# Block inverse of a chunked RWKV-7 scan: 128-row transposes and copies, and PSUM columns of its own for the third stage

## The chip, the cores and the metric

The kernel runs on one core of a Trainium2 chip. The metric is device time in microseconds for one execution. Every program is timed several times and the median counts. One further execution is recorded by the hardware profiler. It gives the trace from which all durations below are read.

## The reference, cut to what matters

One step of a two-layer trunk. Layer 0 is attention (differential heads and latent heads); layer 1 is a bidirectional RWKV-7 time mixing with 32 heads of width 64, over 512 latent tokens and 128 context tokens. The change touches layer 1 alone. Its recurrence, for each direction:

```python
def step(s, inp):
    r_t, w_t, k_t, v_t, kk_t, a_t = inp
    sa = jnp.einsum('bhij,bhj->bhi', s, -kk_t)
    s = s * w_t[:, :, None, :] + sa[..., None] * (kk_t * a_t)[:, :, None, :] + v_t[..., None] * k_t[:, :, None, :]
    return s, jnp.einsum('bhij,bhj->bhi', s, r_t)
...
s_fin, ys = lax.scan(step, s0, xs, reverse=reverse)
```

The kernel works on chunks of 64 tokens. Inside a chunk the `sa` terms of all tokens depend on each other through a strictly lower triangular 64x64 matrix, so each chunk and head needs the inverse of a unit lower triangular 64x64 matrix. That inverse is what the changed function computes.

## The kernel before, in words

Layer 1 runs over 16 pairs of heads and, for each, two passes u = 0 and 1: 32 **units**. A unit holds, in its 128 rows, both directions (64 rows each) for five chunks of two heads, so ten 64x64 inverses per direction.

For each unit the generator `unit` (L1488) writes out the work of three neighbouring units in one order. First comes the sequential scan of unit n (`stage_c`, L1299), then the list `P2` (L1482): the inverse of unit n+1 (`inv`), transposes of its keys (`bk`), its values (`pre`), a bonus term, and the Gram matrices of unit n+2 (`a2`, matmul L1125, evacuated by VectorE into GG at L1129). Between these steps `fill` lets the big projections (`project_steps`, matmul L126) advance by a few matmuls, as cover for the waits. The instruction order of TensorE is the order of this program text (`manual_schedule`, L1552); a scheduler orders VectorE, ScalarE and GpSimd by their priorities and its own estimate of time. Inverse steps are written with a raised priority (`urgent`, L1463).

The inverse (`stage_inv`, L1240) starts from 16x16 blocks already inverted on VectorE (tile DD) and has four steps, all of whose matmuls write into one PSUM tile, CC (128 rows x 2 banks x 512 columns):

- stage 1: 80 matmuls (L1260) into columns PB (416:496), then two VectorE operations (L1263) that make t16;
- stage 2: 80 matmuls (L1269) into columns PA (256:416), the inverses of the 32x32 diagonal blocks. Of each group of 64 rows the first 32 hold the upper block, the last 32 the lower. The upper ones are transposed by VectorE (L1274, two instructions of 32 rows, into DD), the lower ones copied by ScalarE into the result tile xd (L1276, two of 32 rows);
- stage 3: 40 matmuls (L1282) into the lower rows of the same columns PA. ScalarE then copies these (L1285, twice 32 rows) and the upper blocks (L1287, twice 32 rows);
- stage 4: 40 matmuls (L1291) into the upper rows of PA, then two ScalarE copies with scale -1 (L1294).

The scan of the next unit reads xd (matmul L1343).

CC is allocated at L848, right after layer 0's output projection and the modulation of layer 1's input. That modulation ends with VectorE operations at L818, which write h0lo, half of the input of every layer 1 projection. CC is first used as the accumulator of a projection: L911 sets up three projections lg[0], lg[1] (into tiles of the pool pj) and lg[2] (into CC), and L913 runs their weight chunks in turn, while VectorE is still writing the last parts of h0lo. A weight chunk is 12 pairs of matmuls of 320 columns. Each chunk of weights is split into two parts, whi by ScalarE (L100) and wlo by GpSimd (L101); wlo has two buffers.

Of the kernel before, what the change touches and what calls it, by code (L numbers as in the profile page):

```python
# [14 lines left out]
AF = mybir.ActivationFunctionType  # L15
# [38 lines left out]
def kernel(  # L54
# [5 lines left out]
    act, dve, pool, pe = nc.scalar, nc.vector, nc.gpsimd, nc.tensor  # L60
# [779 lines left out]
    with ExitStack() as l1:  # L840
# [5 lines left out]
        pc = tc.alloc_tile_pool(name="pc", bufs=1, space=PSUM)  # L846

        CC = pc.tile([128, 2, 512], F32, name="CC")  # L848

        def c3(t):  # L850
            return t.rearrange("p (c t) -> p c t", t=64)
# [7 lines left out]
        nlow = b1.tile([128, 1], F32, name="nlow")  # L859
        dve.tensor_reduce(out=nlow, in_=i32[:, 16:32], axis=AX.X, op=ALU.add, negate=True)  # L860
        i32b = i32.rearrange("p (o t) -> p o t", o=1).to_broadcast([128, 10, 32])
        t16 = b1.tile([128, 10, 32], F32, name="t16")
# [11 lines left out]
        for t in Xds:  # L874
            dma(out=t.rearrange("p c -> (p c)").rearrange("(p c) -> p c", p=128),
                in_=xds[0][:, 0:5, :].rearrange("p q t -> p (q t)"))
# [9 lines left out]
        def shifted(alloc, wd, n, ti, pt=None, lead=False):  # L886
            if pt is None:
                pt = pj.tile([128, 1024], F32, tag="pj", name="pj")
            yield from project_steps([pt[:, 512 - HT:512], pt[:, 512:512 + HT]], wd, KT, n, h1hi, h1lo, HALVES, 4, 0, lead)
            X = pt[:, 512 - HT:512 + HT]  # L890
            out = alloc()
            act.activation(out=out, in_=X[:n], func=AF.Copy, scale=c0[:n, ti:ti + 1])
            for a, b, _ in SEGS:
                dve.scalar_tensor_tensor(out=out[:, a + 1:b], in0=X[:n, a:b - 1], scalar=V("mu0", ti)[:n],
                                         in1=out[:, a + 1:b], op0=ALU.mult, op1=ALU.add)
                dve.scalar_tensor_tensor(out=out[:, a:b - 1], in0=X[:n, a + 1:b], scalar=V("mu1", ti)[:n],
                                         in1=out[:, a:b - 1], op0=ALU.mult, op1=ALU.add)

            return out
# [8 lines left out]
        def ring(pool_, tag, shape=(128, T), dt=F32, **kw):  # L908
            return lambda: pool_.tile(list(shape), dt, tag=tag, name=tag, **kw)

        lg = [shifted(ring(u1, tag), w_l1[64 + j], 128, 64 + j, pt, j < 2)  # L911
              for j, (tag, pt) in enumerate((("az", None), ("kk", None), ("kzs", CC.rearrange("p b c -> p (b c)"))))]
        for j in (0, 1, 0, 1, 2) + (0, 1, 2) * 3:  # L913
# [124 lines left out]
        def halves_of(u):  # L1038
            return [(hf ^ u, HT * hf, HT * hf + HT, 5 * hf, 5 * hf + 5) for hf in range(2)]
# [200 lines left out]
        def stage_inv(i, u):  # L1240
            un = units[(i, u)]
            zh = halves_of(u)
            G = un.GAq
            xd = un.xd = xds[u]
            Dn, D = un.DD[:, 0], un.DD[:, 1]
            grp = [(64 * z + 32 * m, 32 * m, 2 * ca) for z, _, _, ca, _ in zh for m in range(2)]
            PA, PB = CC[:, :, 256:416], CC[:, :, 416:496]

            def blk(o, q):
                return PA[o:o + 32, q // 5, 32 * (q % 5):32 * (q % 5) + 32]  # L1250

            def pa(o):
                return PA[o:o + 32].rearrange("p b (q t) -> p b q t", t=32)

            def b2(t):
                return t.rearrange("p (b q) t -> p b q t", b=2)

            for q in range(10):
                for o, col, q0 in grp:
                    pe.matmul(PB[o:o + 32, q // 5, 16 * (q % 5):16 * (q % 5) + 16], G[o:o + 32, q0 + q, col:col + 32],  # L1260
                              Dn[o:o + 32, q, 0:16], start=True, stop=True, tile_position=(o, o))
            for k in range(2):
                dve.scalar_tensor_tensor(out=t16[:, 5 * k:5 * k + 5, 0:16],  # L1263
                                         in0=PB[:, k].rearrange("p (q t) -> p q t", t=16), scalar=nlow,
                                         in1=i32b[:, 0:5, 0:16], op0=ALU.mult, op1=ALU.add)
            yield
            for q in range(10):
                for o, col, q0 in grp:
                    pe.matmul(blk(o, q), t16[o:o + 32, q, :], D[o:o + 32, q, :],  # L1269
                              start=True, stop=True, tile_position=(o, o))  # L1270
            xn = un.DD[:, 0]
            for o, col, q0 in grp:
                if col == 0:
                    dve.transpose(out=b2(xn[o:o + 32]), in_=pa(o))  # L1274
                else:
                    act.activation(out=b2(xd[o:o + 32, :, col:col + 32]), in_=pa(o), func=AF.Copy)  # L1276
            yield
            t32 = xn
            for q in range(10):
                for z, a, b, ca, cb in zh:  # L1280
                    o = 64 * z
                    pe.matmul(blk(o + 32, q), G[o:o + 32, 2 * ca + q, 32:64], xn[o:o + 32, q, :],  # L1282
                              start=True, stop=True, tile_position=(o, o + 32))
            for o in (0, 64):
                act.activation(out=b2(t32[o + 32:o + 64]), in_=pa(o + 32), func=AF.Copy)  # L1285
            for o in (0, 64):
                act.activation(out=b2(xd[o:o + 32, :, 0:32]), in_=pa(o), func=AF.Copy)  # L1287
            yield
            for q in range(10):
                for o in (0, 64):  # L1290
                    pe.matmul(blk(o, q), t32[o + 32:o + 64, q, :], xd[o + 32:o + 64, q, 32:64],  # L1291
                              start=True, stop=True, tile_position=(o + 32, o))
            for o in (0, 64):
                act.activation(out=b2(xd[o:o + 32, :, 32:64]), in_=pa(o), func=AF.Copy, scale=-1.0)  # L1294
            yield

        carry = {}
# [1 line left out]
        def stage_c(i, u):  # L1299
# [3 lines left out]
            Yn = un.Yn = u1.tile([128, 5, 2, 64], F32, tag="yz", name="Yn")  # L1303
            Ys = CC[:, :, 192:512].rearrange("p h (s d) -> p s h d", d=64)

# [13 lines left out]
            for s in range(5):  # L1319
                loc = (s, 4 - s)  # L1320
                cgs = (un.ca[0] + loc[0], un.ca[1] + loc[1])
                if u == 0 and s == 0:
                    dma(out=ZS[:, 0, :], in_=state[0, i])
                    dma(out=ZS[:, 3, :], in_=state[1, i])
                    S = ZS[:, 0:2, :]
                C = CC[:, :, 0:64]
                pu, pn = (CC[:, 1, 64:192], CC[:, 0, 64:192]), CC[:, 0, 64:192]
                if s:
# [159 lines left out]
        def unit(n):  # L1488
# [5 lines left out]
            sub, a1, kk = of(stage_a3, n + 1), of(stage_a1, n + 2), kk_of(n + 2)  # L1494
            gn = stage_gn(*seq[n - 1]) if n else iter(())
            bonus, inv = of(stage_bonus, n), urgent(of(stage_inv, n + 1))
            P1 = {-1: [kk], 2: [gn, sub, kk], 4: [a1], 5: [kk, sub], 7: [a1], 8: [gn], 10: [a1], 11: [gn], 13: [a1], 15: [bonus]}
            w1 = 0
# [27 lines left out]
        def prologue():  # L1526
            quota[1] = 1.0
            need(proj_k, 0)
            script(dict(kk=kk_of(0), a1=of(stage_a1, 0)),
                   (("a1", 9), ("a1", 9), ("kk", 9), ("kk", 7), ("a1", 7), ("kk", 5), ("a1", 0)))  # L1530
            need(proj_r, 0)
            all_(of(stage_e, 0))
            fill(36)
            a1, bk = of(stage_a1, 1), of(stage_bk, 0)
            a2 = of(stage_a2, 0)
            for g, w in ((a2, 4), (a1, 6), (a2, 4), (a1, 6), (a2, 4)):
                step(g)
                fill(w)
            all_(a2, of(stage_a3, 0))
            for g, w in ((bk, 6), (bk, 6), (a1, 8), (bk, 6)):  # L1540
                step(g)
                fill(w)
            all_(a1, bk)
            need(proj_v, 0)
            all_(of(stage_e, 1))
            of(stage_v, 0)
            script(dict(pre=of(stage_pre, 0), inv=urgent(of(stage_inv, 0)), a2=of(stage_a2, 1)),
                   (("pre", 6), ("pre", 32), ("inv", 3), ("a2", 6), ("inv", 3), ("inv", 3),
                    ("a2", 6), ("pre", 3), ("inv", 3), ("pre", 3), ("a2", 6)))
            need(proj_r, 1)  # L1550
# [139 lines left out]
```

## Time and profile before

| | us |
|---|---|
| median of 3 runs | 3641.58 (3637.04 to 3645.55) |
| profiled execution, own time | 3634.34 |
| its span, first to last instruction | 3632.5 |
| TensorE busy | 3426.5 (94%) |
| VectorE busy | 2141.9 (59%) |
| ScalarE busy | 1632.0 (45%) |
| GpSimd busy | 1190.0 (33%) |
| mean granted TensorE clock | 0.988 of full speed |

PE is TensorE's matmul stream and PEld its weight loads, DVE is VectorE, ACT is ScalarE, POOL is GpSimd, SP issues DMAs. In a timeline row the columns are start, duration, engine, line, operation, output tile <- input tiles, shapes, count; a bracket at the end gives how long the engine had been idle before it and who ended that wait. Rows of neighbouring equal instructions are merged, so a duration there runs from the start of the first to the end of the last.

### The profile page before, as it was taken

The page shows a single profiled execution, that of the slowest core. Times are in us where ns is not written, and L with a number is a line of the kernel's source. Part 1 is how long each engine was busy: PE and PEld are TensorE (multiplying, and loading weights), DVE is VectorE, ACT ScalarE, POOL GpSimd, SP SyncE. Part 2 cuts the span into 40 slices and gives each one's busy share as a digit, 9 for nine tenths or more (in the row PEclk, how much of TensorE's full clock was granted, in tenths as well). Part 3 has the DMA queues.
Part 4 walks back from the last instruction along what each step waited for, and adds up shares of the span by engine and source line. Part 5 has one row for each costly group of instructions (what it writes and reads, how often), then busy time and mean ns, then how long its engine had stood idle before and what let it go on. Part 6 is the DMA issues. An engine that isn't in the chain of part 4 may idle for free. (4 is left out here: it accounts for less than half of the span.)

```text
span 3632.5 us, 84033 instructions
## 1 busy us (share of the span) xinstructions
PE 3426.5 (94%) x34432; PEld 2997.9 (83%) x34432; DVE 2141.9 (59%) x4249; ACT 1632.0 (45%) x3342; POOL 1190.0 (33%) x1094
## 2 busy tenths in 40 slices
PE   8999999999999989999999999999999999999998
PEld 4788889988888879898877778778777787888898
DVE  3356655666666584555666666666676666665402
ACT  3244443444444422444544545545545455555422
POOL 1222112222222344542333323333233333333444
PEclk9999999999999999999999999999999999999999
DMA  9623433333333364332222222222222322323534
GB/s 332 220 69 103 124 96 113 106 110 108 107 107 110 119 221 162 106 94 64 69 72 62 68 70 69 67 67 69 68 68 66 74 65 68 75 70 92 172 96 145
DMA packets 388610, 376.23 MB, mean 104 GB/s; under 512 B 200512, under 2 KB 242560, under 8 KB 388224
## 3 DMA queue, kind: packets, MB, share of 16 engines
q1 hardware_dynamic: 388224, 370.86, 34.7%
q8 instruction: 270, 4.42, 0.5%
q14 instruction: 116, 0.95, 0.1%
HBM read 328.51 MB, written 42.24 MB: 102 GB/s over the span
## 5 line engine op out<-in xcount | busy, mean ns | idle before, releaser
L101 POOL TENSOR_TENSOR wlo<-raw,whi 128x512 fp32r<-128x512 f32 (+1 forms) x628 | 861.2, 1372 | 1976.3 <-PE pj L126 1254.4
L126 PE MATMUL pj<-h0hi,wlo 128*128 128x320 f32 x4448 | 1085.2, 323 | 20.2 <-POOL wlo L101 20.2
L126 PE MATMUL pj<-h0hi,whi 128*128 128x320 f32 x4448 | 1081.0, 322 | 2.3 <-ACT whi L100 1.8
L126 PE MATMUL pj<-h0lo,whi 128*128 128x320 f32 x4448 | 1075.4, 321 | 2.3 <-DVE h0lo L101 1.6
L126 PEld LDWEIGHTS pj<-h0hi,wlo 128*128 128x128 f32 x4448 | 744.2, 190 | 56.4 <-POOL wlo L101 24.8
L126 PEld LDWEIGHTS pj<-h0hi,whi 128*128 128x128 f32 x4448 | 743.1, 190 | 36.0 <-issue 7.9
L126 PEld LDWEIGHTS pj<-h0lo,whi 128*128 128x128 f32 x4448 | 745.7, 190 | 30.6 <-issue 8.2
L100 ACT ACTIVATE whi<-raw 128x512 fp32r<-128x512 f32 (+1 forms) x628 | 390.7, 622 | 743.1 <-PE pj L126 402.3
L200 DVE SCALAR_TENSOR_TENSOR aacc<-araw,scs,aacc 128x512 f32<-128x512 f32 x480 | 409.5, 901 | 16.6 <-DMA araw<-in_dram 15.8
L364 DVE TENSOR_REDUCE nm<-S 128x1 f32<-128x768 f32 (+1 forms) x120 | 98.3, 819 | 255.2 <-PE S L376 255.1
L1345 ACT ACTIVATE UV<-CC 64x128 f32<-64x128 f32 x160 | 43.1, 269 | 335.6 <-PE CC L1343 306.8
L724 DVE SCALAR_TENSOR_TENSOR x<-pj,mod,xr 128x512 f32<-128x512 f32 (+2 forms) x68 | 33.2, 524 | 248.1 <-PE pj L126 242.6
L367 ACT ACTIVATE P<-S,nm 128x768 f32<-128x768 f32 (+1 forms) x120 | 95.1, 792 | 166.7 <-DVE nm L364 166.0
L1129 DVE TENSOR_TENSOR GG<-gram,con 128x512 f32<-128x512 f32 (+1 forms) x192 | 107.4, 595 | 73.6 <-PE gram L1125 73.2
L1125 PE MATMUL gram<-AR,BK 64*128 64x128 f32 x1280 | 114.0, 292 | 18.0 <-DVE GG L1129 13.2
L1125 PEld LDWEIGHTS gram<-AR,BK 64*128 64x128 f32 x1280 | 90.3, 189 | 42.7 <-DVE GG L1129 24.1
L1061 PE MATMUL plo<-lr,lw 96*128 96x320 f32 x256 | 103.7, 487 | 5.7 <-DMA lr<-lorad 4.7
L566 PE MATMUL po<-PT,vt 128*128 128x128 f32 x800 | 103.2, 276 | 0.1
L566 PEld LDWEIGHTS po<-PT,vt 128*128 128x128 f32 x800 | 98.0, 191 | 4.2 <-issue 2.5
L1359 DVE TENSOR_TENSOR S<-CC,S 128x128 f32<-128x128 f32 (+1 forms) x112 | 29.9, 267 | 118.8 <-PE CC L1310 78.6
L1335 DVE SCALAR_TENSOR_TENSOR rhs<-CC,MV 128x128 f32<-128x128 f32 x160 | 45.8, 286 | 69.9 <-PE CC L1333 69.6
L1343 PEld LDWEIGHTS CC<-rhs,xd 64*64 64x64 f32 x1280 | 49.8, 133 | 42.8 <-DVE rhs L1335 20.8
(338 smaller groups left out, 5209.1 us busy)
## 6 DMA issues: line engine op xcount, KB each, us to landing
raw<-in_dram SPq DMA_DIRECT2D x612, 256.0 KB
araw<-in_dram SPq DMA_DIRECT2D x384, 256.0 KB
lr<-lorad SPq DMA_DIRECT2D x128, 120.0 KB
Ld<-GG SPq DMA_DIRECT2D x64, 160.0 KB
lw<-in_dram SPq DMA_DIRECT2D x128, 48.0 KB
x<-in_dram SPq DMA_DIRECT2D x16, 320.0 KB
xr<-in_dram SPq DMA_DIRECT2D x16, 320.0 KB
DD<-Xd SPq DMA_DIRECT2D x32, 160.0 KB
```

What stands on the lines that cost most here:

```text
L100: act.activation(out=hi, in_=src, func=AF.Copy)
L101: (lo_eng or pool).tensor_tensor(out=lo, in0=src, in1=rf(hi), op=ALU.subtract)
L126: pe.matmul(p[:n, 0:b - a], w, x[:, kk ^ flip, a:b], start=(kk == order[0] and i == 0), stop=(kk == order[-1] + kc - 1 and i == 2))
L200: dve.scalar_tensor_tensor(out=acc[:, s], in0=raw, scalar=scs[:, k, s:s + 1], in1=acc[:, s], op0=ALU.mult, op1=ALU.add)
L364: dve.tensor_reduce(out=nm, in_=S[:, 0:nk], axis=AX.X, op=ALU.max, negate=True)
L367: act.activation(out=P[:, 0:nk], in_=S[:, 0:nk], func=AF.Exp, bias=nm, accum_out=l)
L566: pe.matmul(po[:, 0:128], H.vt[:, kt, :], PT[:, j, :], start=(j == 0), stop=(j == n - 1))
L1061: pe.matmul(ps[:, 0:HT], lw, lo, start=True, stop=True)
L1125: pe.matmul(ps[:, j * 128:(j + 1) * 128], BK[hs, c + j, :, :].rearrange("p a t -> p (a t)"), AR[hs, c + j, :, :].rearrange("p a t -> p (a ...
L1129: dve.tensor_tensor(out=GG[:, c:c + n, h, :], in0=ps[:, 0:n * 128].rearrange("p (j t) -> p j t", t=128), in1=maskg.rearrange("p (o t) -> p ...
L1335: dve.scalar_tensor_tensor(out=rhs.rearrange("p (h d) -> p h d", h=2), in0=C, scalar=-1.0, in1=un.MV[:, s, :].rearrange("p (h d) -> p h d" ...
L1343: pe.matmul(pu[z][o:o + 64, hs], xd[o:o + 64, 2 * loc[z] + h, :], rhs[o:o + 64, hs], start=True, stop=True)
```

## The change

Four things change. The second-stage transposes become one instruction over all 128 rows and the second-stage copies one, so rows that were not needed are processed too (the lower blocks are transposed into rows of DD that are overwritten later, the upper ones copied into a part of xd that is overwritten by stage 4). Stage 3 writes to columns PT (0:160) of CC instead of PA; its result and the upper blocks are copied by one 128-row instruction each, and the minus sign moves to the first of them. As the second copy now also writes 32 rows per direction of xd that must be zero, two GpSimd memsets of 32 rows set them back. Stage 4's result is copied by one 128-row instruction. Since rows of PT that no matmul has written are now read, the whole of CC is set to zero once, where it is allocated.

```diff
         CC = pc.tile([128, 2, 512], F32, name="CC")
+        dve.memset(CC, 0.0)
...
-            PA, PB = CC[:, :, 256:416], CC[:, :, 416:496]
+            PA, PB, PT = CC[:, :, 256:416], CC[:, :, 416:496], CC[:, :, 0:160]
...
-            xn = un.DD[:, 0]
-            for o, col, q0 in grp:
-                if col == 0:
-                    dve.transpose(out=b2(xn[o:o + 32]), in_=pa(o))
-                else:
-                    act.activation(out=b2(xd[o:o + 32, :, col:col + 32]), in_=pa(o), func=AF.Copy)
+            xn = t32 = un.DD[:, 0]
+            dve.transpose(out=b2(xn), in_=p4(PA))
+            act.activation(out=b2(xd[:, :, 32:64]), in_=p4(PA), func=AF.Copy)
             yield
-            t32 = xn
             for q in range(10):
                 for z, a, b, ca, cb in zh:
                     o = 64 * z
-                    pe.matmul(blk(o + 32, q), G[o:o + 32, 2 * ca + q, 32:64], xn[o:o + 32, q, :],
+                    pe.matmul(blk(PT, o + 32, q), G[o:o + 32, 2 * ca + q, 32:64], xn[o:o + 32, q, :],
                               start=True, stop=True, tile_position=(o, o + 32))
-            for o in (0, 64):
-                act.activation(out=b2(t32[o + 32:o + 64]), in_=pa(o + 32), func=AF.Copy)
-            for o in (0, 64):
-                act.activation(out=b2(xd[o:o + 32, :, 0:32]), in_=pa(o), func=AF.Copy)
+            act.activation(out=b2(t32), in_=p4(PT), func=AF.Copy, scale=-1.0)
+            act.activation(out=b2(xd[:, :, 0:32]), in_=p4(PA), func=AF.Copy)
+            for o in (32, 96):
+                pool.memset(xd[o:o + 32, :, 0:32], 0.0)
             yield
...
-            for o in (0, 64):
-                act.activation(out=b2(xd[o:o + 32, :, 32:64]), in_=pa(o), func=AF.Copy, scale=-1.0)
+            act.activation(out=b2(xd[:, :, 32:64]), in_=p4(PA), func=AF.Copy)
```

The remaining lines of the diff only rename: `blk` takes the columns as an argument, and `p4` replaces `pa`.

The instructions move at two places. The first is ScalarE's row around the inverse of one unit, where L1276, L1285, L1287 and L1294 of the kernel before are L1273, L1280, L1281 and L1289 of the changed one; the bracket names what an instruction waits for. Before:

```order
L1276 ACTIVATE xd_14636<-CC 32x10x32 [waits DVE_49]
L1200 ACTIVATE BKn<-pbk 128x512 [waits PE_49]
L1276 ACTIVATE xd_14636<-CC 32x10x32 [waits DVE_49]
L1222 ACTIVATE UV<-pvt 64x512 [waits PE_49]
L1222 ACTIVATE UV<-pvt 64x512
L100 ACTIVATE whi<-raw 128x512 [waits DMAHW4_49,PE_49,Pool_49]
L1285 ACTIVATE DD<-CC 32x320 [waits DMAHW5_49,PE_49]
L1285 ACTIVATE DD<-CC 32x320
L1287 ACTIVATE xd_14636<-CC 32x10x32 x2
```

And now:

```order
L1273 ACTIVATE xd_14637<-CC 128x10x32 [waits DVE_49]
L1201 ACTIVATE BKn<-pbk 128x512 [waits PE_49]
L1223 ACTIVATE UV<-pvt 64x512 [waits PE_49]
L1223 ACTIVATE UV<-pvt 64x512
L100 ACTIVATE whi<-raw 128x512 [waits DMAHW4_49,PE_49,Pool_49]
L1280 ACTIVATE DD<-CC 128x320 [waits DMAHW5_49,PE_49]
L1281 ACTIVATE xd_14637<-CC 128x10x32
```

The second copy of stage 2, which stood behind another operation and waited for VectorE once more, is gone; the first keeps its place and its wait. The first matmul of stage 3 waits for ScalarE in both programs.

The second place is the start of layer 1 on TensorE, where lg[2] begins to accumulate in CC. Before, its first full run of matmuls stands right behind the first chunks of lg[0] and lg[1]:

```order
L126 MATMUL pj<-h0hi,whi 128x320
L126 MATMUL pj<-h0lo,whi 128x320
L126 MATMUL pj<-h0hi,wlo 128x320
L126 MATMUL CC<-h0lo,whi 128x320
L126 MATMUL CC<-h0hi,wlo 128x320 x2
L126 MATMUL CC<-h0hi,whi 128x320 x2
L126 MATMUL CC<-h0lo,whi 128x320 x2
```

Now the second chunks of lg[0] and lg[1] (24 pairs) and the first two pairs of lg[0]'s third come first, and behind them two chunks of lg[2] in a row:

```order
L126 MATMUL pj<-h0lo,whi 128x320 x2
L126 MATMUL pj<-h0hi,wlo 128x320 x2
L126 MATMUL pj<-h0hi,whi 128x320 x2
L126 MATMUL pj<-h0lo,whi 128x320 x2
L126 MATMUL CC<-h0hi,whi 128x320 x2
L126 MATMUL CC<-h0lo,whi 128x320 x2
L126 MATMUL CC<-h0hi,wlo 128x320 x2
```

On VectorE the new memset that these matmuls wait for (its order in the changed kernel) stands behind the very last of the h0lo operations:

```order
L818 SCALAR_TENSOR_TENSOR h0lo<-x_12180,mod_89,h0hi 128x192
L818 SCALAR_TENSOR_TENSOR h0lo<-x_12180,mod_89,h0hi 128x128
L849 MEMSET CC 128x1024
L855 MEMSET scm 128x640
L859 TENSOR_REDUCE i_14638<-con 128x32
```

So lg[2], which before needed only its weights and the first parts of h0, now begins after all of h0lo.

## Rows read from the trace of the kernel before

**Rows 1.** The page's head and its first section: span, and busy time of each engine.

```profile
span 3632.5 us, 84033 instructions
PE 3426.5 (94%) x34432; PEld 2997.9 (83%) x34432; DVE 2141.9 (59%) x4249; ACT 1632.0 (45%) x3342; POOL 1190.0 (33%) x1094
```

**Rows 2.** Busy time by stretch, for the stretch from the first to the last inverse: stretch and its length, then busy us and count of PE, PEld, DVE, ACT, POOL, the granted clock, DMA share and GB/s.

```profile
1632.00:3362.00 1730.00, 1631.02 (x22927) 1384.14 (x22916) 1116.74 (x2655) 880.66 (x1924) 566.56 (x633) 0.99 0.27 70
```

**Rows 3.** Who TensorE waited for over the whole run: total us, times, longest us.

```profile
PE CC L1282 <- ACT xd L1276: 26.6, 27, 2.8
...
PE gram L1125 <- DVE GG L1129: 13.2, 21, 1.3
...
PE CC L1291 <- ACT xd L1287: 7.0, 14, 1.1
```

**Rows 4.** Groups of instructions by form, on VectorE and ScalarE in the stretch 1630 to 3360: busy us, mean ns of one, idle before them and who ended it.

```profile
L1274 DVE STREAM_TRANSPOSE DD<-CC 32x320 f32<-32x320 f32 x64 | 32.5, 508 | 26.8 <-ACT xd L1276 20.3 <-PE CC L1269 5.5
L1276 ACT ACTIVATE xd<-CC 32x320 f32<-32x320 f32 x64 | 27.4, 429 | 39.3 <-DVE DD L1274 38.2
```

**Rows 5.** Timeline of one unit around stage 2's evacuation and stage 3, VectorE, ScalarE and TensorE.

```profile
2352.98 0.52 DVE L1274 STREAM_TRANSPOSE DD<-CC 32x320 f32<-32x320 f32 x1
...
2353.53 0.43 ACT L1276 ACTIVATE xd<-CC 32x320 f32<-32x320 f32 x1 [2.71 <-DVE DD L1274]
...
2353.99 0.51 DVE L1274 STREAM_TRANSPOSE DD<-CC 32x320 f32<-32x320 f32 x1 [0.49 <-ACT xd L1276]
...
2354.60 0.43 ACT L1276 ACTIVATE xd<-CC 32x320 f32<-32x320 f32 x1
...
2355.08 0.82 PE L1282 MATMUL CC<-DD,GG 32*32 32x32 f32 x40 [0.80 <-ACT xd L1276]
```

**Rows 6.** The three units with the longest wait before stage 3: stage 3 on TensorE, and for the longest of them the two copies of stage 2 on ScalarE.

```profile
2742.95 0.82 PE L1282 MATMUL CC<-DD,GG 32*32 32x32 f32 x40 [1.99 <-ACT xd L1276]
...
3070.98 0.43 ACT L1276 ACTIVATE xd<-CC 32x320 f32<-32x320 f32 x1
...
3072.55 0.43 ACT L1276 ACTIVATE xd<-CC 32x320 f32<-32x320 f32 x1
3073.03 0.82 PE L1282 MATMUL CC<-DD,GG 32*32 32x32 f32 x40 [2.79 <-ACT xd L1276]
...
3178.75 0.82 PE L1282 MATMUL CC<-DD,GG 32*32 32x32 f32 x40 [1.96 <-ACT xd L1276]
```

**Rows 7.** Timeline of one unit from stage 3 to stage 4, TensorE and ScalarE.

```profile
2188.58 0.82 PE L1282 MATMUL CC<-DD,GG 32*32 32x32 f32 x40 [0.40 <-ACT xd L1276]
2190.50 0.87 ACT L1285 ACTIVATE DD<-CC 32x320 f32<-32x320 f32 x2
2191.38 0.86 ACT L1287 ACTIVATE xd<-CC 32x320 f32<-32x320 f32 x2
2192.30 0.82 PE L1291 MATMUL CC<-xd,DD 32*32 32x32 f32 x40 [1.01 <-ACT xd L1287]
```

**Rows 8.** Groups by form again: a transpose on VectorE and a copy on ScalarE over 128 rows.

```profile
L1189 DVE STREAM_TRANSPOSE DD<-DD 128x320 f32<-128x320 f32 x31 | 15.7, 507 | 39.8 <-DMA DD<-Xd 39.8
L1200 ACT ACTIVATE BKn<-pbk 128x512 f32<-128x512 f32 x62 | 36.6, 591 | 11.0 <-PE pbk L1199 10.3
```

**Rows 9.** GpSimd around the same place of a unit with u = 0 (timeline), with ScalarE's last copy there, and the group of an existing GpSimd memset.

```profile
2964.25 0.87 ACT L1287 ACTIVATE xd<-CC 32x320 f32<-32x320 f32 x2
2965.32 1.64 POOL L101 TENSOR_TENSOR wlo<-raw,whi 128x512 fp32r<-128x512 f32 x1 [3.75 <-issue]
L1148 POOL MEMSET Xp<- 104x256 f32 x30 | 9.7, 324 | 39.4 <-DMA Xd<-Xp 34.8 <-DVE S L1368 4.7
```

**Rows 10.** The same unit behind stage 3: the key transposes on TensorE, the first VectorE operation behind the transposes of stage 2, and the Gram matmul that waited for VectorE.

```profile
2964.51 0.38 PE L1199 MATMUL pbk<-con,BK 128*128 128x128 f32 x2
2964.93 0.89 DVE L1092 TENSOR_TENSOR BK<-kk,az 128x320 f32<-128x320 f32 x2 [3.31 <-PE pbk L1199]
2976.91 1.16 PE L1125 MATMUL gram<-AR,BK 64*128 64x128 f32 x14 [0.37 <-DVE GG L1129]
```

**Rows 11.** The start of layer 1: TensorE where lg[2] and the second and third chunks of lg[0] start, and VectorE's last h0lo operations and the memsets behind them.

```profile
1513.09 0.31 PE L126 MATMUL CC<-h0lo,whi 128*128 128x320 f32 x1
...
1516.59 0.46 PE L126 MATMUL pj<-h0hi,whi 128*128 128x320 f32 x2
...
1523.63 0.46 PE L126 MATMUL CC<-h0hi,whi 128*128 128x320 f32 x2
...
1527.94 0.46 PE L126 MATMUL pj<-h0hi,whi 128*128 128x320 f32 x2
1523.64 3.47 DVE L818 SCALAR_TENSOR_TENSOR h0lo<-x,mod,h0hi 128x192 fp32r<-128x192 f32 x8
1528.19 0.59 DVE L867 MEMSET xd<- 128x640 f32 x1
```

**Rows 12.** Two idle times of TensorE and the stretches behind them (stretch and length, PE busy us and count, granted clock, DMA share, GB/s).

```profile
1502.50 1.43 PE L778 MATMUL pj<-sq,ones 128*128 128x320 f32 x2 [2.98 <-ACT sq L730]
1503.00:1508.30 5.30, 5.30 (x20) 0.50 0.10 35
1569.51 0.99 PE L1061 MATMUL plo<-lr,lw 96*128 96x320 f32 x2 [2.10 <-DMA lr<-lorad]
1569.50:1573.50 4.00, 3.99 (x15) 0.57 0.15 43
```

More of the change, by code (lines that the diff above doesn't have):

```diff
@@ L1246, in stage_inv, with blk, p4 @@
             grp = [(64 * z + 32 * m, 32 * m, 2 * ca) for z, _, _, ca, _ in zh for m in range(2)]
-            PA, PB = CC[:, :, 256:416], CC[:, :, 416:496]
[L1249 to L1253, printed above, removed]
+            PA, PB, PT = CC[:, :, 256:416], CC[:, :, 416:496], CC[:, :, 0:160]
+            def blk(P, o, q):
+                return P[o:o + 32, q // 5, 32 * (q % 5):32 * (q % 5) + 32]
+            def p4(P):
+                return P.rearrange("p b (q t) -> p b q t", q=5)
             def b2(t):
@@ L1262, in stage_inv @@
             for k in range(2):
-                dve.scalar_tensor_tensor(out=t16[:, 5 * k:5 * k + 5, 0:16],
-                                         in0=PB[:, k].rearrange("p (q t) -> p q t", t=16), scalar=nlow,
+                dve.scalar_tensor_tensor(out=t16[:, 5 * k:5 * k + 5, 0:16], in0=p4(PB)[:, k], scalar=nlow,
                                          in1=i32b[:, 0:5, 0:16], op0=ALU.mult, op1=ALU.add)
@@ L1268, in stage_inv @@
                 for o, col, q0 in grp:
-                    pe.matmul(blk(o, q), t16[o:o + 32, q, :], D[o:o + 32, q, :],
+                    pe.matmul(blk(PA, o, q), t16[o:o + 32, q, :], D[o:o + 32, q, :],
                               start=True, stop=True, tile_position=(o, o))
-            xn = un.DD[:, 0]
-            for o, col, q0 in grp:
-                if col == 0:
-                    dve.transpose(out=b2(xn[o:o + 32]), in_=pa(o))
-                else:
-                    act.activation(out=b2(xd[o:o + 32, :, col:col + 32]), in_=pa(o), func=AF.Copy)
+            xn = t32 = un.DD[:, 0]
+            dve.transpose(out=b2(xn), in_=p4(PA))
+            act.activation(out=b2(xd[:, :, 32:64]), in_=p4(PA), func=AF.Copy)
             yield
-            t32 = xn
             for q in range(10):
@@ L1290, in stage_inv @@
                 for o in (0, 64):
-                    pe.matmul(blk(o, q), t32[o + 32:o + 64, q, :], xd[o + 32:o + 64, q, 32:64],
+                    pe.matmul(blk(PA, o, q), t32[o + 32:o + 64, q, :], xd[o + 32:o + 64, q, 32:64],
                               start=True, stop=True, tile_position=(o + 32, o))
-            for o in (0, 64):
-                act.activation(out=b2(xd[o:o + 32, :, 32:64]), in_=pa(o), func=AF.Copy, scale=-1.0)
+            act.activation(out=b2(xd[:, :, 32:64]), in_=p4(PA), func=AF.Copy)
             yield
```

## The prediction

> **What bounds the kernel now.** I read the page's busy times first: TensorE's matmul stream is busy for 3426.5 of 3632.5 us, so at most 206 us of the span are idle there, and no other engine passes 59% [rows 1]. The change removes no matmul, so it can only act on TensorE's waits. Next, the stretch of the inverses, 1632 to 3362: 1631 of 1730 us busy, 99 us idle [rows 2]. Which waits these are says the list of TensorE's waits: the longest of all is stage 3 of the inverse waiting for ScalarE's copy to xd, 26.6 us in 27 of the 32 units; stage 4's wait on the same engine is 7.0 us in 14 [rows 3]. Those two lines, 33.6 us, are all that the edit of the inverse can win.
>
> Why stage 3 waits is seen in the timeline of a unit [rows 5]: transpose, copy, transpose, copy go in turns between VectorE and ScalarE although they take different rows of CC. The second transpose sat idle 0.49 us for the first copy, and over all units transposes sat idle 20.3 us for copies and copies 38.2 us for transposes [rows 4]. From the first transpose's start to the last copy's end it took 2354.60 + 0.43 - 2352.98 = 2.05 us, and stage 3 started 0.05 us later.
>
> **Stage 2's evacuation.** Removed: one transpose of 0.51 us, one copy of 0.43 us and the hand-overs between them, per unit. The chain that is left ends with the first copy: 2353.53 + 0.43 = 2353.96 instead of 2355.03, so 1.07 us fall away in this unit [rows 5]. Where other operations stand between the two copies on ScalarE more falls away: in the unit with the longest wait 3072.55 - 3070.98 = 1.57 us of 2.79 [rows 6]. The rule for one unit is the smaller of its wait and of what falls away. Only three units wait clearly longer than that (2.79, 1.99 and 1.96, [rows 6]; in the last two I get 1.69 that falls away by the same subtraction). Unit by unit I get 24.8 of the 26.6 us. The least, with 1.07 everywhere, would be about 22.
>
> This needs 128 rows to cost what 32 did. A transpose over 128 rows of 320 columns takes 0.507 us where the one of 32 rows takes 0.508, the input being in SBUF instead of PSUM; a 128-row copy of 512 columns out of PSUM takes 0.59 [rows 4, 8], and one of 32 rows and 320 columns 0.43. I take both unchanged. The other end would be time by rows, four times as long; it is a rival below.
>
> The order rows of the change show that stage 3 still waits for ScalarE, not only for the transpose, although it now writes columns which that copy doesn't read. So I give the columns of their own no gain: the copy's end, not the transpose's, stays the point from which stage 3 starts. Here the Trainium skill has a rule (PSUM — Partial Sum Buffer, section "PSUM bank collisions raise a hardware error"): guard PSUM by bank and group of 32 rows, not by address. PT lies in the same two banks as PA, so by that rule new columns free nothing, as I take it. The rule would let the old transposes and copies, in different groups of 32 rows, run side by side; the rows show them in turns, so the trace is stricter than the page. If addresses counted, stage 3 would win the remaining 1.8 us of its 26.6 at most.
>
> **Stages 3 and 4.** ScalarE's four copies (0.87 + 0.86 us, [rows 7]) become two, 0.86 us less ahead of stage 4; with the minus sign moved nothing else changes. But TensorE now also comes up to about 1 us earlier, while ScalarE is only 0.43 us earlier where it was held by its own queue (in [rows 7] it began 1.1 us after stage 3 had ended). Unit by unit that leaves 2.5 us of stage 4's 7.0, so 4.5 are won; the bounds are 0 and 7.0. Stage 4's last copies have no reader until the next scan and win nothing.
>
> **The memsets on GpSimd.** Two per unit, 64 in all, each near the 0.32 us of the memset of 256 columns [rows 9]: some 0.8 us per unit with 320 columns. They wait for the copy of the upper blocks; behind them in the queue stand the splits hl and wlo, for whose results TensorE waits. In the rows GpSimd was idle for 3.75 us right there, and the last copy ended at 2965.12, 0.2 us ahead of the next split [rows 9]. Now that copy ends at least 1.7 us earlier, so the memsets fit. I count 0. Uncovered they would delay a split by 0.8 us, 26 us over all units if nothing hid it; the double buffer of wlo does, so I hold 3 us for the bad end.
>
> **The memset of CC.** This is where the change costs. Before, TensorE worked without CC's being set: in the timeline [rows 11] lg[2]'s first chunk ran until 1516.59, the next chunks of lg[0] and lg[1] until 1523.63 (24 pairs in 7.04 us, 0.293 a pair), and lg[2]'s second chunk until 1527.94. So by 1527.94 four chunks were done, as VectorE's h0lo came to its end at 1523.64 + 3.47 = 1527.11. Now the memset stands behind that last h0lo, and 1024 columns at the rate of the memset of 640 (0.59 us, [rows 11]) are 0.94 us: CC is free at about 1528.2. Until then TensorE's order allows only two of the four chunks and two pairs. The other two chunks, 7.04 us, are done later; less two pairs (0.59), plus 1528.2 - 1527.94: 6.7 us lost. From there on TensorE is short of time, not of data, so I see nothing that gives this back.
>
> The new idle time, about 7 us in pieces, should also bring the clock down: after idle times of 2.98 and 2.10 us it stood at 0.50 for 5.3 us and at 0.57 for 4 us, the 1.2 GHz level for most of that [rows 12]. That cost 0.50 x 5.3 = 2.7 and 0.43 x 4 = 1.7 us. I take 2.2. The loss at this place is 8.9 us, with bounds from 4 (a part covered, no drop of the clock) to 12.
>
> **The sum.** -24.8 - 4.5 + 6.7 + 2.2 = -20.4 us. The profiled execution took 3634.34 us, so 3613.9; the median of the timed runs is 7.24 us above it, and the same step there gives 3641.58 - 20.4 = 3621 us.
>
> **What is late next.** When TensorE passes stage 3 earlier, it could run into VectorE: the Gram matmuls waited 13.2 us for GG [rows 3]. In the unit of [rows 10] VectorE's run of operations that ends with GG began only after the key transposes on TensorE (idle 3.31 us until then), and these stand behind stage 3 in TensorE's order. So that run starts earlier by the same time, and the wait should stay about what it was. In units whose VectorE is held by ScalarE's evacuation of a gate, ScalarE is also relieved (eight copies become four).
>
> **Rivals.**
>
> First, the start of layer 1 costs nothing, because TensorE finds cover or the memset comes early. For it: 7 us are little beside 206 of idle. Against it: the order of both engines is fixed, and no other matmul stands ahead of lg[2]. It gives 3641.6 - 29.3 = 3612. Chance 0.13.
>
> Second, half of the gain in the units comes back as waits for GG or for ScalarE further down. For it: VectorE is busy for 65% of the stretch [rows 2] and waits for GG exist. Against it: rows 10, as said. -14.7 + 8.9 gives 3636. Chance 0.14.
>
> Third, on the slower side: VectorE is the true bound between stage 3 and the Gram matmuls. Then all of the gain is waited out in front of gram, and the 8.9 us at the start of layer 1 remain: 3650. It decides the sign once more than 20.4 of the 29.3 us come back, that is if GG's waits grow from 13.2 to above 33. For and against as for the second. Chance 0.07.
>
> Fourth, the single instruction costs by rows. The copy ahead of stage 3 then ends 1.53 + 1.29 us later than I assume, and the two ahead of stage 4 take 3.44 instead of 1.73 us. Stage 3's wait grows by about 1.4 in each of 27 units (38 us), stage 4's by 1.7 in 14 (24 us), with the 8.9 that is 3712. The rows of 128 that cost no more speak against it [rows 8]. Chance 0.03.
>
> **How the numbers follow.** My forecast has the remaining 0.63, its own range 3613 to 3629: the bounds of stage 3 (22 to 26.6), of stage 4 (0 to 7) and of the start (4 to 12). About 0.2%, 7 us, is what a measurement of this kernel can tell from no change. Below 3634.3 lie nearly all of the forecast, the first rival and a little of the second: faster 0.79. Within 7 us lie most of the second, some of the third and a little of the forecast: 0.13. Slower: 0.08, the rest of the third and the fourth. A range of 3609 to 3637 leaves out the third, the fourth and the outer ends.
>
> **What would show it.** In the changed profile stage 3's wait should be below 4 us and stage 4's below 4; one transpose of about 0.51 and four copies of 0.43 us a unit; GpSimd's splits without new waits of TensorE; a memset on CC of about 0.9 us near 1528, and in front of the first matmul into CC an idle TensorE, followed by some microseconds at half clock; the first inverse about 9 us later than before, and the last one about 20 earlier. It would be wrong if the transposes or copies are longer, if gram's wait for GG grows by more than a few microseconds, or if TensorE stays busy between 1513 and 1528.

## The result and the profile after

| | before | changed |
|---|---|---|
| median, us | 3641.19 (3637.04 to 3645.55, 4 runs) | 3612.46 (3601.49 to 3617.26, 4 runs) |
| ratio | | 0.9911, 95% interval 0.9896 to 0.9926 |
| profiled execution, own time | 3634.34 | 3616.01 |
| its span | 3632.5 | 3614.2 |

The kernel became faster by 28.7 us in the medians and by 18.3 us between the two profiled executions. The forecast was 20.4 us for both, 3621 us on the median. Repeated twice, each time beside fresh runs of the kernel before (below), the change was worth 24.5 and 32.2 us; the mean of the three is 28.5. So the sign was right, and 3612.46 lies within the wide range of 3609 to 3637, but half a microsecond outside the forecast's own range of 3613 to 3629: the gain is some 8 us larger than the sum.

The page's head after the change, as in [rows 1]:

```profile
span 3614.2 us, 84002 instructions
PE 3429.2 (95%) x34432; PEld 3004.6 (83%) x34432; DVE 2121.4 (59%) x4218; ACT 1564.7 (43%) x3214; POOL 1217.8 (34%) x1158
```

TensorE's work is the same, ScalarE has 128 instructions fewer, VectorE 31 fewer (32 transposes gone, one memset new) and GpSimd 64 more.

TensorE's waits after, answering [rows 3] (total us, times, longest us):

```profile
PE pj L126 <- POOL wlo L101: 26.8, 16, 5.3
...
PE gram L1126 <- DVE GG L1130: 12.3, 21, 2.6
...
PE gram L1126 <- ACT MV L1238: 5.4, 10, 1.2
...
PE CC L1278 <- ACT xd L1273: 1.2, 2, 1.0
...
PE CC L1287 <- ACT xd L1281: 0.4, 1, 0.4
```

Stage 3 (now L1278) waited 26.6 us and waits 1.2; stage 4 (L1287) waited 7.0 and waits 0.4. The Gram matmuls' wait for GG is 12.3 after 13.2: VectorE took nothing of the gain back.

Groups by form after, in the stretch of the inverses, answering [rows 4]: the transpose on VectorE, three of the four copies on ScalarE, the memsets on GpSimd.

```profile
L1272 DVE STREAM_TRANSPOSE DD<-CC 128x320 f32<-128x320 f32 x32 | 16.2, 507 | 4.0 <-PE CC L1269 3.7
```

```profile
L1273 ACT ACTIVATE xd<-CC 128x320 f32<-128x320 f32 x32 | 13.8, 430 | 34.5 <-DVE DD L1272 34.4
L1281 ACT ACTIVATE xd<-CC 128x320 f32<-128x320 f32 x32 | 13.6, 425 | 0.0
L1280 ACT ACTIVATE DD<-CC 128x320 f32<-128x320 f32 x32 | 13.5, 422 | 1.4 <-PE CC L1278 1.4
```

```profile
L1283 POOL MEMSET xd<- 32x320 f32 x64 | 22.9, 358 | 48.8 <-ACT xd L1281 47.6
```

128 rows cost what 32 did, 507 against 508 ns and 430 against 429, so for these two operations the number of rows does not set the time. VectorE's transposes no longer wait for ScalarE (20.3 us of idle before).

The evacuation in one unit after, answering [rows 5]: VectorE, ScalarE, TensorE.

```profile
2350.13 0.50 DVE L1272 STREAM_TRANSPOSE DD<-CC 128x320 f32<-128x320 f32 x1
```

```profile
2350.66 0.44 ACT L1273 ACTIVATE xd<-CC 128x320 f32<-128x320 f32 x1 [2.59 <-DVE DD L1272]
...
2353.12 0.42 ACT L1280 ACTIVATE DD<-CC 128x320 f32<-128x320 f32 x1
2353.44 0.43 ACT L1281 ACTIVATE xd<-CC 128x320 f32<-128x320 f32 x1
```

```profile
2351.47 0.82 PE L1278 MATMUL CC<-DD,GG 32*32 32x32 f32 x40
...
2354.68 0.82 PE L1287 MATMUL CC<-xd,DD 32*32 32x32 f32 x40
```

From the transpose's start to the copy's end it now takes 2350.66 + 0.44 - 2350.13 = 0.97 us instead of 2.05, and stage 3 comes later than that (2351.47) with no wait: TensorE has projection matmuls until then. Stage 4 has no wait either.

The start of layer 1 after, answering [rows 11]: TensorE's rows with idle in front of them, the first matmul into CC and the one behind lg[2]'s two chunks, then VectorE's last h0lo and the memset, then the split on GpSimd that came late.

```profile
1516.13 0.90 PE L126 MATMUL pj<-h0hi,wlo 128*128 128x320 f32 x2 [1.07 <-POOL wlo L101]
...
1523.25 0.55 PE L126 MATMUL pj<-h0hi,wlo 128*128 128x320 f32 x2 [1.84 <-POOL wlo L101]
...
1526.91 0.56 PE L126 MATMUL pj<-h0hi,whi 128*128 128x320 f32 x2 [0.47 <-ACT whi L100]
...
1527.61 0.46 PE L126 MATMUL CC<-h0hi,whi 128*128 128x320 f32 x2
...
1534.65 0.46 PE L126 MATMUL pj<-h0hi,wlo 128*128 128x320 f32 x2
```

```profile
1521.99 3.46 DVE L818 SCALAR_TENSOR_TENSOR h0lo<-x,mod,h0hi 128x192 fp32r<-128x192 f32 x8
...
1525.66 0.91 DVE L849 MEMSET CC<- 128x1024 f32 x1 [0.21 <-issue]
```

```profile
1521.05 2.14 POOL L101 TENSOR_TENSOR wlo<-raw,whi 128x512 fp32r<-128x512 f32 x1 [4.97 <-PE pj L126]
```

lg[2]'s two chunks run from 1527.61 to 1534.65, 7.04 us in one piece, all behind the memset, where before one of them was done by 1516.59 and the other by 1527.94. TensorE did not stand idle in front of CC itself: it ran out of weights before that. GpSimd's split waited 4.97 us for matmuls that still read a buffer of wlo, and TensorE then 1.84 us for the split; as I read it, the other buffer was held by lg[2]'s chunk, which was not to run before the memset. From the end of the last h0lo (1525.45, before 1527.11) to the first inverse TensorE has 717 matmuls instead of 668; the two chunks are 48 of them. The changed kernel, then the kernel before (stretch and length, PE busy us and count, granted clock, DMA share, GB/s):

```profile
1525.45:1634.52 109.07, 105.21 (x717) 1.00 0.33 96
```

```profile
1527.11:1631.82 104.71, 99.97 (x668) 0.98 0.34 97
```

The clock around the start of layer 1, answering [rows 12] (same columns):

```profile
1513.00:1516.00 3.00, 0.85 (x4) 1.00 0.28 87
1516.00:1520.00 4.00, 3.87 (x16) 0.57 0.20 66
1520.00:1524.00 4.00, 2.16 (x15) 1.00 0.00 0
```

Behind 2.15 idle us in three, the granted clock was 0.57 for 4 us, near the 1.2 GHz level.

### The profile page after: what moved, and what is told of

It is laid out like the page before. It is cut to its first block, busy times and chain, and to the rows that moved or that the text cites. A ratio compares the mean times of both kernels' runs of the same rounds, so it can differ in the third digit from the quotient of the medians.

```text
span 3614.2 us, 84002 instructions
## 1 busy us (share of the span) xinstructions
PE 3429.2 (95%) x34432; PEld 3004.6 (83%) x34432; DVE 2121.4 (59%) x4218; ACT 1564.7 (43%) x3214; POOL 1217.8 (34%) x1158
## 5 line engine op out<-in xcount | busy, mean ns | idle before, releaser
L1126 PE MATMUL gram<-AR,BK 64*128 64x128 f32 x1280 | 116.6, 296 | 19.3 <-DVE GG L1130 12.3
```

The source lines that it names most:

```text
L1126: pe.matmul(ps[:, j * 128:(j + 1) * 128], BK[hs, c + j, :, :].rearrange("p a t -> p (a t)"), AR[hs, c + j, :, :].rearrange("p a t -> p (a ...
```

## Experiments

The runs came in three groups of four kernels, each group beside the kernel before on one chip. The three medians of the kernel before were 3647.72 (17 runs, first group), 3649.99 (20 runs, second) and 3649.24 us (11 runs, third); differences in us below are of medians of one group.

**The change again** (no edit).

> The changed kernel once more, on the chip and beside the runs that the three other kernels are compared with. Theory: the waits of stages 3 and 4 are gone (26.6 + 7.0 us before) and the start of layer 1 pays some 3 to 9 us, so 20 to 29 us less than before, ratio 0.992 to 0.9945. Rival (part of the first result was the luck of few runs): ratio near 0.995 or above.

Measured: 3623.24 us, ratio 0.9931 (0.9918 to 0.9944), 24.5 us less.

**The memset of CC alone.** The kernel before and one line:

```diff
         CC = pc.tile([128, 2, 512], F32, name="CC")
+        dve.memset(CC, 0.0)
```

> The kernel before with nothing but the memset of CC. Theory (the memset makes TensorE run two chunks later): 6.7 us for the two chunks and about 2 for the clock, ratio 1.0018 to 1.0025, the first inverse about 9 us later in the profile. Rival (the order finds cover at the start of layer 1): 0 to 3 us, ratio 1.000 to 1.001, the first inverse at most 3 us later.

Measured: 3656.51 us, ratio 1.0026 (1.0012 to 1.0040), 8.8 us more. The memset is not free; its cost is near the 8.9 us of the sum, with an interval of 4 to 15 us.

**The memset moved behind lg[2].** The changed kernel, with only PT's columns set to zero, after the loop over lg's chunks:

```diff
-        dve.memset(CC, 0.0)
...
+        dve.memset(CC[:, :, 0:160], 0.0)
```

> The changed kernel, with the memset behind the projection that uses CC, and only of the 160 columns of PT. Theory: TensorE's order at the start of layer 1 is that of before, so the cost of the memset is gone: 7 to 9 us faster than the changed kernel. Rival (the memset costs little): within 3 us of the changed kernel.

Measured: 3615.35 us, ratio 0.9911 (0.9893 to 0.9928), 7.9 us less than the changed kernel beside it. It is also a shorter memset, but the long one takes only 0.91 us; so the price is the memset's place. The intervals of the two kernels overlap; a repeat of both (below) gives 8.5 us.

**Stage 2's evacuation alone.** The kernel before with one transpose and one copy over 128 rows in stage 2; stages 3 and 4 and CC as before.

```diff
-            for o, col, q0 in grp:
-                if col == 0:
-                    dve.transpose(out=b2(xn[o:o + 32]), in_=pa(o))
-                else:
-                    act.activation(out=b2(xd[o:o + 32, :, col:col + 32]), in_=pa(o), func=AF.Copy)
+            pa4 = PA.rearrange("p b (q t) -> p b q t", q=5)
+            dve.transpose(out=b2(xn), in_=pa4)
+            act.activation(out=b2(xd[:, :, 32:64]), in_=pa4, func=AF.Copy)
```

> The kernel before with stage 2's two transposes and two copies merged over 128 rows, nothing else. Theory (stage 3's wait is the chain transpose, copy, transpose, copy, and TensorE's idle time is what counts): stage 3's wait falls from 26.6 to about 2 us, stage 4's stays at 7 or grows by a few, 20 to 25 us less, ratio 0.993 to 0.9945. Rival (half of it comes back as waits of the Gram matmuls): 10 to 13 us less, and the wait of gram for GG grows from 13 to about 25 us.

Measured: 3623.05 us, ratio 0.9933 (0.9920 to 0.9946), 24.7 us less. Its waits, stage 4 on L1289 and stage 3 on L1280:

```profile
PE CC L1289 <- ACT xd L1285: 12.8, 21, 1.5
...
PE CC L1280 <- ACT xd L1274: 1.1, 2, 0.9
```

Stage 3's wait is gone without columns of its own. But stage 4's grew from 7.0 to 12.8 us: TensorE comes to it earlier and finds ScalarE at its four copies. The Gram matmuls' wait for GG is 12.5 us, so the rival falls.

**Stages 3 and 4 alone**, with the late memset; stage 2 as before. Stage 3 writes to PT, stage 4's result is copied by one instruction as in the changed kernel, and between them:

```diff
+            act.activation(out=b2(t32), in_=p4(PT), func=AF.Copy, scale=-1.0)
+            act.activation(out=b2(xd[:, :, 0:32]), in_=p4(PA), func=AF.Copy)
+            for o in (32, 96):
+                pool.memset(xd[o:o + 32, :, 0:32], 0.0)
```

> Only stages 3 and 4 are changed (result of stage 3 in PT, two copies over 128 rows with the minus sign moved, two memsets on GpSimd); stage 2 keeps its two transposes and two copies in turns, and the memset is on PT's columns only, behind the last chunk of lg. Theory (the two terms add): stage 3's wait stays at 26 us, stage 4's falls from 7 to about 0, the time falls by 4 to 8 us, ratio 0.998 to 0.999. Rival (columns of their own also free stage 3 from the copies): stage 3's wait falls by 5 us or more and the time by over 12 us.

Measured: 3644.35 us, ratio 0.9986 (0.9971 to 1.0001), 5.6 us less, hardly to be told from nothing. Stage 3's wait stays, though its result has columns of its own:

```profile
PE CC L1281 <- ACT xd L1276: 27.2, 28, 2.2
```

**The order of stage 2's operations.** The kernel before with both transposes written first, then both copies:

```diff
             for o, col, q0 in grp:
                 if col == 0:
                     dve.transpose(out=b2(xn[o:o + 32]), in_=pa(o))
-                else:
+            for o, col, q0 in grp:
+                if col:
```

> The kernel before with stage 2's four operations written in another order, both transposes and then both copies, nothing merged. Theory (two things were paid, the turns and the second pair of operations): the two transposes take 1.0 us, the two copies behind them 0.87, so stage 3 starts some 0.1 to 0.2 us earlier a unit than with the turns (2.05 us); its wait falls by 3 to 6 us and the time by as much, ratio 0.998 to 0.999. Rival (the turns alone were the price, and rows of 32 would run side by side): the wait falls by 15 us or more, ratio 0.995 or less.

Measured: 3638.73 us, ratio 0.9965 (0.9952 to 0.9978), 11.3 us less: between the two. One unit, VectorE, ScalarE and stage 3:

```profile
2355.83 1.03 DVE L1274 STREAM_TRANSPOSE DD<-CC 32x320 f32<-32x320 f32 x2
```

```profile
2356.96 0.87 ACT L1277 ACTIVATE xd<-CC 32x320 f32<-32x320 f32 x2 [3.27 <-DVE DD L1274]
```

```profile
2357.88 0.82 PE L1283 MATMUL CC<-DD,GG 32*32 32x32 f32 x40 [0.73 <-ACT xd L1277]
```

ScalarE still begins behind the second transpose, and the whole takes 2.0 us after 2.05. In the profile stage 3's wait fell to 15.4 us, and stage 4's rose to 20.4; together 35.8, so by the waits nothing is won. This profile is of the slowest of the nine runs (3642.31), and its stretch of the inverses is as long as before's, so it can't show where the 11 us come from; that stays open. By the medians the order alone is worth about half of what the merging is.

**Without GpSimd's memsets**, twice. The late memset with the upper blocks copied by two instructions of 32 rows:

```diff
-            act.activation(out=b2(xd[:, :, 0:32]), in_=p4(PA), func=AF.Copy)
-            for o in (32, 96):
-                pool.memset(xd[o:o + 32, :, 0:32], 0.0)
+            for o in (0, 64):
+                act.activation(out=b2(xd[o:o + 32, :, 0:32]), in_=p4(PA[o:o + 32]), func=AF.Copy)
```

> As the late memset, but the copy of the upper blocks is again two copies of 32 rows, which need no memsets on GpSimd. Theory (the memsets are hidden): the same as the late memset within 3 us, stage 4's wait up by 2 to 5 us for one more copy of 0.43 us in front of it, the wait for wlo as it was (24 us). Rival (the memsets delay the splits behind them): the wait for wlo falls by 4 us or more and the time by 3 to 8 us.

Measured: 3606.75 us, ratio 0.9886 (0.9868 to 0.9904). That looked 9 us better than the late memset, but on another chip; so both ran once more side by side:

> The late memset with two copies of 32 rows in place of one of 128 and two memsets on GpSimd, once more. Theory (the memsets on GpSimd are hidden): the same as the late memset within 3 us. Rival (they delay the splits behind them, as the first run of it suggested): 5 to 10 us faster than the late memset of this call, with a wait for wlo that is 3 us smaller or more.

Measured: 3608.39 us, ratio 0.9888 (0.9870 to 0.9905), and the late memset beside it:

> The late memset once more. Theory: 6 to 9 us faster than the changed kernel of the same call, ratio 0.990 to 0.991, 104 to 107 us from the last h0lo to the first inverse. Rival (the place of the memset is worth nothing): within 3 us of the changed kernel.

Measured: 3608.53 us, ratio 0.9891 (0.9876 to 0.9905). No difference, so the first gap lay between chips or in the scatter of few runs. Stage 4's wait is 3.0 us without the memsets and 0.4 with them, as one more copy stands in front of it; so the memsets may still cost up to some 3 us that this pair can't show. Beside these two ran the changed kernel:

> The changed kernel once more, beside three others of the same chip. Theory (the memset at the start of layer 1 costs 6 to 9 us and the clock gives some back in the stretch of the inverses): ratio 0.992 to 0.994; in its profile 109 to 113 us from the end of the last h0lo to the first inverse, TensorE idle for 70 to 75 us between the first and the last inverse and busy for 1601 to 1606 us there. Rival (the gain beyond the forecast was chance of the first runs): ratio 0.9945, 20 us.

Measured: 3617.03 us, ratio 0.9915 (0.9901 to 0.9929), 32.2 us less than before, a little more than the theory allowed, and 8.5 us more than the late memset.

**Stage 3's result in its old place**, twice. First the changed kernel with PA for PT and no memset of CC:

```diff
-                    pe.matmul(blk(PT, o + 32, q), G[o:o + 32, 2 * ca + q, 32:64], xn[o:o + 32, q, :],
+                    pe.matmul(blk(PA, o + 32, q), G[o:o + 32, 2 * ca + q, 32:64], xn[o:o + 32, q, :],
...
-            act.activation(out=b2(t32), in_=p4(PT), func=AF.Copy, scale=-1.0)
+            act.activation(out=b2(t32), in_=p4(PA), func=AF.Copy, scale=-1.0)
```

> The changed kernel with stage 3's result back in its old place, the lower rows of PA, and all else as changed; no column stays unwritten, so the memset of CC is gone too. Theory (the columns of their own win nothing, the memset costs 8 us): ratio as the late memset, 0.991, within 0.0015, stage 3's wait about 1 us. Rival (the columns of their own are what freed stage 3): stage 3's wait is 2 to 10 us again, ratio 0.993 to 0.994.

Measured: 3609.56 us, ratio 0.9889 (0.9869 to 0.9908); stage 3's wait was 1.1 us. This kernel changes the computation: its last copy takes all rows of PA and so writes stage 3's result over the lower diagonal blocks of xd; only its time and its waits are used. The second version keeps them, with two copies of 32 rows at the end and for the upper blocks, and needs no memset at all:

```diff
-            act.activation(out=b2(xd[:, :, 32:64]), in_=p4(PA), func=AF.Copy)
+            for o in (0, 64):
+                act.activation(out=b2(xd[o:o + 32, :, 32:64]), in_=p4(PA[o:o + 32]), func=AF.Copy)
```

> Stage 3's result in the lower rows of PA as before, nothing set to zero on any engine; stage 2 with one transpose and one copy over 128 rows, the copy of the result over 128 rows with the minus sign, the upper blocks and the last copies two of 32 rows each. Theory (columns of their own win nothing, so none is needed): the same as the late memset without GpSimd's memsets within 3 us, ratio 0.988 to 0.991, stage 3's wait about 1 us, stage 4's 1 to 4. Rival (the columns of their own matter for stage 3): stage 3's wait 5 us or more, ratio 0.992 or above.

Measured: 3613.06 us, ratio 0.9900 (0.9882 to 0.9919), 4.7 us above the version without GpSimd's memsets beside it. That is more than the 3 us of the theory, but the intervals overlap widely. Its waits for stage 4 and stage 3:

```profile
PE CC L1285 <- ACT xd L1281: 2.5, 7, 0.8
...
PE CC L1277 <- ACT xd L1272: 1.3, 2, 1.2
```

The columns of their own do nothing for stage 3; what they buy is that the last copy can take 128 rows.

## Where the gain came from

Medians give what a part is worth, the profiles where it sits. This table cuts each profile at three points that all kernels have: the end of the last h0lo of layer 1, the first and the last inverse (first row of stage 1). TensorE's busy time is that of the same 22,521 or 22,522 matmuls; idle is length minus busy.

| profile of | last h0lo to first inverse | first to last inverse | idle there | busy there | last inverse to end |
|---|---|---|---|---|---|
| before | 104.7 | 1705.4 | 98.9 | 1606.5 | 295.3 |
| memset of CC alone | 111.4 | 1717.8 | 105.3 | 1612.5 | 297.5 |
| stages 3 and 4 alone | 103.8 | 1705.1 | 94.0 | 1611.1 | 295.6 |
| other order | 105.9 | 1705.4 | 99.7 | 1605.7 | 299.8 |
| stage 2 alone | 104.5 | 1687.4 | 84.4 | 1602.9 | 297.5 |
| changed | 109.1 | 1678.8 | 73.0 | 1605.8 | 300.9 |
| changed, second | 112.6 | 1673.4 | 71.8 | 1601.6 | 300.3 |
| changed, third | 113.4 | 1674.2 | 73.1 | 1601.1 | 301.1 |
| late memset | 106.6 | 1671.6 | 70.5 | 1601.1 | 300.5 |
| late memset, second | 105.6 | 1677.9 | 74.7 | 1603.2 | 297.1 |

The stretch's row for the kernel before, the memset alone, stage 2 alone, the changed kernel and the third run of it (PE's columns alone):

```profile
1631.82:3337.23 1705.41, 1606.52 (x22521) 0.99 0.27 70
```

```profile
1645.09:3362.89 1717.80, 1612.54 (x22521) 0.99 0.28 69
```

```profile
1631.48:3318.85 1687.37, 1602.93 (x22521) 0.99 0.29 70
```

```profile
1634.52:3313.32 1678.80, 1605.76 (x22521) 0.99 0.28 71
```

```profile
1646.40:3320.58 1674.18, 1601.08 (x22521) 0.99 0.28 71
```

Two profiles have the whole of the old code of the inverses (before, memset alone) and five the whole of the new (changed, late memset). Means of new less old: idle 72.6 - 102.1 = -29.5, busy 1602.6 - 1609.5 = -6.9, from the last inverse to the end 300.0 - 296.4 = +3.6. The first column with the memset at CC's allocation is 111.6 in the mean of four, without it 105.0 in the mean of the other six and of the four further profiles (103.9 to 106.0): +6.6. Sum: -26.2 us; 2.3 of the 28.5 us are not located.

## Why the prediction was right, and where it was wrong

The gain was 28.5 us in the mean instead of 20.4. The step that failed is a term that the sum put at nothing, the clock in the stretch of the inverses; beside it the shares of stage 2 and of stages 3 and 4 were off in opposite directions, which cancels.

**Stage 2: right in time, in part by luck.** Forecast -24.8, all of it idle time; alone it gave -24.7 us, and stage 3's wait fell from 26.6 to 1.1. But 5.8 us of that came back as stage 4's wait. In the table TensorE's idle time with stage 2 alone is 14.5 us less than before (17.7 less than the mean of the two profiles with the old inverses), and its busy time 3.6 us (6.6) less, which the sum did not have. So the time was met although less idle time went than summed. One transpose of 0.51 and copies of 0.43 us came as said, so the fourth rival (time by rows) falls. That stage 3 still waits for ScalarE's copy, and that columns of their own win nothing, is shown from both sides: with them but the old stage 2 the wait was 27.2 us; without them but with stage 2 merged it was 1.1 (stage 2 alone), 1.1 and 1.3 us (result in its old place). The Trainium skill (PSUM — Partial Sum Buffer, section "PSUM bank collisions raise a hardware error") agrees: by it, accesses to one bank and one group of 32 rows collide even at different addresses. It also says that engines in different groups of 32 rows of a bank may work side by side; this program's traces don't show that, as the copies of rows 32 to 63 began 0.10 us behind the transposes even where all transposes stood first (2356.96 after 2356.86).

**Stages 3 and 4: the size was off.** The step said "Unit by unit that leaves 2.5 us of stage 4's 7.0, so 4.5 are won". 0.4 us were left. Worse, its ceiling of 7.0 was the wait of the old kernel; with stage 2 merged alone that wait is 12.8, so the edit of stages 3 and 4 removes 12.4 us of it. By time it is worth 3623.05 - 3615.35 = 7.7 us on top of stage 2, or 16.0 if the late memset's second run, of another chip, is set against it (40.7 - 24.7). Before stage 2 is merged it is worth 5.6. The 5.8 us that stage 4 takes back from stage 2's gain were missing on the other side, so in the sum of both waits the error is small: 33.6 to 1.6 us is -32.0 against -29.3.

**The clock in the stretch of the inverses: the step that failed.** The sum ended with "-24.8 - 4.5 + 6.7 + 2.2": it charged the clock for the new idle time at the start of layer 1 and gave nothing back for the idle time removed. Idle fell by 29.5 us, as summed (29.3), and the same matmuls were also busy for 6.9 us less, about what the forecast was short (8 us by the medians). Summed over windows of 4 us, what the granted clock lay under 1.00 made 12.0 and 18.8 us between the first and the last inverse with the old inverses, and 13.7, 10.3, 8.3, 9.0 and 10.2 with the new: 5.1 us less in the mean. The other profiles agree: TensorE is busy for 1605.7 to 1612.5 us in the four profiles whose stage 2 is not merged, and for 1599.8 to 1605.8 in all ten where it is. Against the profile of before alone both differences would be smaller (26.3 idle, 3.9 busy), and the two profiles with the old inverses lie 12 us apart; the size is thus known to some microseconds only. No run changed the clock alone, so that the clock is the cause of the shorter busy time is read from these sums and not shown by an experiment.

**The memset of CC: right in size, not in every detail.** Forecast 8.9; measured 8.8, 7.9 and 8.5 by medians, 6.6 in the profiles up to the first inverse. It took 0.91 us, as foreseen, and lg[2]'s two chunks stood behind it. The idle time came in pieces ahead of it, in front of wlo's splits and not in front of CC's first matmul, and the half clock came before the memset instead of behind it. The first inverse was only 2.7 us later than in the trace of before, not 9: the last h0lo ended 1.66 us earlier there (1525.45 against 1527.11), and from it to the first inverse this pair shows 4.4 us more where the mean is 6.6.

**GpSimd's memsets: right, to some 3 us.** 0.36 us each, and no gain without them beside the same kernel with them. TensorE's wait for wlo did grow, from 21.8 to 26.8 us, but with the memset of CC alone it is 26.1 and with the late memset 24.1 and 21.4: that growth belongs to CC's memset.

**The end of the program: not in the sum.** The 2,191 matmuls behind the last inverse took 278.5 us after 273.2, at 0.96 of the clock after 0.98, and the idle time there was the same (22.3 and 22.1 us). That gives back 5.6 us in this pair and 3.6 in the table's means. Since the other order of stage 2 has 299.8 us there too, it is not tied to the new inverses; why the clock is lower stays open.

**From the profile to the median.** "The same step there gives" 3621: the sum met the profiled pair within 2.1 us (18.3 against 20.4), but the profiled execution of before was 6.9 us below its median and that of the changed kernel 3.6 above its own. One pair of traces could not show an error of this size; the three pairs of medians and the table's ten traces do.

**The rivals.** The time that came is the first rival's 3612, and its reason is refuted: the start of layer 1 costs 8 to 9 us. The second and third fall with the wait for GG, 12.3 us after 13.2, and no new wait of that size; small ones grew, as the Gram matmuls' wait for MV from 3.4 to 5.4 us.

## What to carry to other kernels

Here an evacuation split by rows cost each piece the time of the whole (508 against 507 ns), and two engines that shared the tile took turns besides: if the surplus rows are harmless, one instruction over 128 rows is the cheaper form. When a wait is removed, look again at the wait behind it, since its old size is no longer the limit of what the next edit can win, and ask what the clock gives back for idle time removed, as you ask what it costs for idle time added. Set a tile to zero behind the last other use of its columns where you can: moving the memset was worth 8 us here.

## What the runs showed that was not expected

- With the same program text up to CC's allocation, the last h0lo of layer 1 ended anywhere from 1525.5 us (changed) to 1539.3 us (result in place) in 14 profiles. About half of the whole gain can hide in that, so a single profile's time of a later event must be read from a nearby event, not from the span's start.
- A memset of 0.91 us on an engine that is not the bottleneck cost about nine times its length. TensorE's matmuls into CC began 1.0 us after it had ended, and what they waited for last was ScalarE's split of weights for the chunk in front of them (1526.91). The memset cost its price through the order: two chunks that had run beside h0lo ran behind it.
